# Pool layer of a four-layer trunk: pooled tokens ahead of their row work, bias unsplit, conditioning units redistributed

## The chip, the cores and the metric

One Trainium2 chip, one NeuronCore. The metric is device microseconds of one launch, the median over runs; the kernel before took 1184.72 us (three runs, 1184.19 to 1185.09).

## The reference

The trunk has four layers over x (256 tokens, 1024 channels), all in float32. Layer i mixes tokens by attention (i = 0, 3), a causal convolution (i = 1) or causal pooling (i = 2), and each mixer is followed by a squared-ReLU MLP of 4096 hidden channels:

```python
h = rmsnorm(x) * (1 + scale_a) + shift_a          # rows of c @ ada_w + ada_b
x = x + gate_g * rmsnorm(mixer(h))
h = rmsnorm(x) * (1 + scale_m) + shift_m
x = x + gate_m * rmsnorm(relu(h @ w1) ** 2 @ w2)
# pooling mixer: four groups of 256 channels, windows 2, 4, 8, 16
pooled = trailing_mean(h, window_g) - h
y = (pooled_g @ w_g + b_g) * pool_scale
```

The adaLN rows (shift, scale and gate of every sub-layer) come from one vector c, so each is a matrix-vector product with 1 MB pieces of ada_w.

## The kernel before, in words

Tokens lie as two tiles t = 0, 1 of 128 tokens. Every float32 weight is split into hi and lo halves that TensorE takes at full rate (ACT casts hi, DVE subtracts to lo: `load`, L173 and L174), and a product is three matmuls, hi·hi, lo·hi and hi·lo (`mm3`, L561 to L565). The program runs, for each layer, a mixer and an MLP (`ffn`, 16 chunks). In the middle of MLP chunk 12 (`mid`) some row work of the next layer is issued, such as `shift_rows` (the shift row is transposed into columns, L328 to L341); the pool layer's is not among it.

Between two sub-layers stands `boundary`, a dependent chain. For each tile: ACT sums the squares of y (L135, two halves), POOL makes the reciprocal root r (L119, L121), DVE scales y by the gate row, which was spread over all partitions (`v<-y,bc_g`, L500), adds it to the residual (L505), ACT sums the squares of that (L135), POOL makes the next r, and DVE multiplies by the scale row (`xa<-xs,bc_a`, L358). Then the tile is transposed for the next product; for the pool layer `tokens` multiplies by r and adds the shift instead (L1140). The helper `line` pins these instructions in program order on their engine. On tile 1 the root's first step runs on DVE (L117).

A gate or scale row reaches all partitions in two DMAs on POOL's queue (`spread`): the row to DRAM (`rowd`, L308), then a broadcast read of 512 KB (`bc_g` or `bc_a`, L311).

The adaLN rows are made from "units", one 1 MB piece `araw` each: on TensorE (four matmuls of 512 columns and their weight loads into the bank `adap`, L256) in mixers and boundaries, or on DVE in MLPs (two multiply-adds of 128x1024, L222), whose sums go through `ada_flush` into `adap`. The eighth unit of a row is followed by two DVE row operations (`row`, L231 and L233 or L235). The tables `MIX` and `FF` say how many units each chunk gets, then how many go into the boundary ahead of the sub-layer, then how many pieces are fetched ahead.

`pool` is a stage of its own after its boundary: the remaining unit, the row spread, four bias matmul pairs from a split bias (`ones_r`, L1175, L1176), four groups of products of the tokens with band matrices (`pT_ps`, L1159; tile 1 has a 16-token overlap with tile 0, L1162), copies to hi and lo (`hT<-pT_ps`, L1167 on ACT, L1168 on DVE), and 48 products into y. The order of instructions on each engine comes from a scheduler that follows the dependences, the pinned lines and the `gate` marks.

Of the kernel before, what the change touches and what calls it, by code (L numbers as in the profile page):

```python
# [20 lines left out]
P = 128  # L21
# [30 lines left out]
def tile_trunk(ctx: ExitStack, tc: tile.TileContext, x, cT, pos, invf, ada_w, ada_bg,  # L52
# [150 lines left out]
    def ada(n, vec=()):  # L203
        for _ in range(n):
# [22 lines left out]
            if k == KT - 1:  # L227
                ada_flush(True)
                row = act.tile([P, 512], F32, tag=f"row{g}", name=f"row{g}",
                               bufs=2 if g == 1 else 1)  # L230
                V.tensor_tensor(row, grp["pt"], bg[:, 0], op=ALU.add)  # L231
                if g == 1:
                    V.tensor_tensor(row, row, bg[:, 1], op=ALU.mult)  # L233
                else:
                    V.scalar_tensor_tensor(row[64:], row[64:], 1.0, bg[64:, 1],  # L235
                                           op0=ALU.add, op1=ALU.mult)
                rows[(i, g)] = row
# [86 lines left out]
    def shift_rows():  # L324
        row = bct["sh"]
# [182 lines left out]
    def boundary(ys, units, planes=None, tokens=None):  # L508
        ada(units)
        last.clear()  # L510
# [12 lines left out]
        if not final:  # L523
            r = rsqrt_eps(*cols(ms))
            if tokens is not None:
                tokens(xa, r)
            else:
                bs = transposed0(xa, r)
# [19 lines left out]
        r = rsqrt_eps(*cols(ms), eng=V)  # L548
        if tokens is not None:
            tokens(scaled(1), r)  # L550
        else:
# [3 lines left out]
            for _ in rest:  # L555
                pass
        gate["pool"] = gate["pow"]
# [557 lines left out]
    def pool(i, head, consts, units, ahead):  # L1115
# [13 lines left out]
        def gain_row(raw):  # L1129
            V.tensor_tensor(raw, raw, psc[0:1, :], op=ALU.mult)  # L1130

        for k in range(2):
            fetch(pool_w[j, k])
        fetch(pool_b[j])
        hs = []

# [6 lines left out]
        head(tokens=tokens)  # L1143
        for k in range(2):
            fetch(w1[i, 0, k])
        ada(units)
        wp = [load(pool_w[j, k], gains) for k in range(2)]
        bh, bl = load(pool_b[j], gain_row)
        prep(rows[(i, 2)])
        shift_rows()  # L1150
        bcast("g", rows[(i, 1)], 0)
        ph, pl = planes()
        for t in range(NT):
            for h in range(2):
                b = bank("h", "pT_ps")
                for k in range(4):
                    kk = 4 * h + k
                    ks = slice(kk * P, (kk + 1) * P)
                    T.matmul(b[:, k * P:(k + 1) * P], hs[t][:, ks], band[:, kk // 2, t, 0:P],  # L1159
                             start=(k == 0), stop=(t == 0), skip_group_check=True)  # L1160
                    if t:
                        T.matmul(b[:, k * P:k * P + 16], hs[0][:, ks],  # L1162
                                 band[:, kk // 2, 0, P:P + 16], start=False, stop=True,
                                 skip_group_check=True)
                o = (slice(None), slice(4 * h, 4 * h + 4), slice(t * P, (t + 1) * P))
                b = b.rearrange("p (k t) -> p k t", k=4)
                gate["act"] = A.copy(ph[o], b)  # L1167
                gate["dve"] = V.tensor_tensor(pl[o], b, ph[o].bitcast(F32), op=ALU.subtract)  # L1168
        gate["free"] = 0
        y = y_banks()  # L1170
        for t in range(NT):
            ts = slice(t * P, (t + 1) * P)
            for n in range(2):
                ns = slice(512 * n, 512 * n + 512)
                T.matmul(y[t][n], ones_r, bh[:, ns], start=True, stop=False, skip_group_check=True)  # L1175
                T.matmul(y[t][n], ones_r, bl[:, ns], start=False, stop=False, skip_group_check=True)  # L1176
            for g in range(4):
                for k in range(2):
# [156 lines left out]
```

## Time and profile before

| what | value |
|---|---|
| median of the runs | 1184.72 us |
| profiled execution | 1186.6 us (span 1184.8 us) |
| TensorE (PE) busy | 1139.5 us, 96% |
| DVE, ACT, POOL busy | 844.7, 644.7, 51.8 us |
| mean granted TensorE clock | 0.98 |
| shares of the chain that ended last | PE 62%, DVE 3%, ACT 2%, POOL 1% |

The profile's times run from the span's start. The stages that matter are, in microseconds of the span: first MLP 161 to 344, convolution 352 to 470, second MLP 482 to 667, pool layer 667 to 689.5, its boundary to 698.6, third MLP 698.6 to 884, second attention to 988, last MLP 1003 to the end. A row of a timeline gives start, duration, engine, line, operation, and in brackets how long the engine had idled and what ended that.

### The profile page before, as it was taken

The numbers are of one execution on the slowest core, as the hardware profiler recorded it, in microseconds if no ns is written. First come the engines' busy times: TensorE is split into PE (matmuls) and PEld (weight loads), VectorE is DVE, ScalarE is ACT, GpSimd is POOL, SyncE is SP. The second block draws the span as 40 slices with busy tenths as digits, with TensorE's granted clock in tenths as the row PEclk, the third lists the DMA queues.
The fourth block names the chain that finished last, engine by engine and source line by source line (L and its number), as shares of the span: only waits on it lengthen the run. The fifth ranks groups of instructions, "written<-read, shape, count | busy, mean of one in ns | idle before, by whom it ended". The sixth has DMA issues, their size and how long they took to land.

```text
span 1184.8 us, 17638 instructions
## 1 busy us (share of the span) xinstructions
PE 1139.5 (96%) x6718; PEld 926.0 (78%) x6718; DVE 844.7 (71%) x1197; ACT 644.7 (54%) x1136; POOL 51.8 (4%) x120
## 2 busy tenths in 40 slices
PE   7899989999999999999999999999998999999997
PEld 4667778888878867778788778887877877888886
DVE  3689678777665664768886877787776986655554
ACT  3355565646653243656565566465556665656553
POOL 1000010000010010100000110000011001000000
PEclk9999989999999998999999999999999999999999
DMA  9878757778727783898887568788636432665560
GB/s 331 305 289 309 290 212 269 290 304 296 278 80 249 258 311 139 294 363 318 335 309 291 231 215 317 286 348 331 240 98 222 157 122 74 232 198 190 184 193 36
DMA packets 73385, 290.03 MB, mean 245 GB/s; under 512 B 9986, under 2 KB 15234, under 8 KB 61012
## 3 DMA queue, kind: packets, MB, share of 16 engines
q1 hardware_dynamic: 70484, 280.44, 64.9%
q0 software_dynamic: 2816, 8.46, 2.2%
q8 instruction: 53, 0.87, 0.3%
q14 instruction: 32, 0.26, 0.1%
HBM read 286.57 MB, written 2.29 MB: 244 GB/s over the span
## 4 chain that ended last, share of the span: by engine, by line
PE 62%; DVE 3%; ACT 2%; issue 1%; POOL 1%; DVEq 0%; POOLq 0%; ACTq 0%; DMA 0%
PE h L596 14%; PE y L561 8%; PE y L565 8%; PE y L564 8%; PE h L599 7%; PE dw_ps L1000 3%; PE adap L256 2%; ACT junk L135 1%; PE pw L578 1%; PE pw L584 1%; PE pw L580 1%; POOL r L121 1%; PE hT_ps L395 1%; PE h L578 1%; PE s_ps L913 1%
## 5 line engine op out<-in xcount | busy, mean ns | idle before, releaser
L174 DVE TENSOR_TENSOR lo<-raw,hi 128x1024 fp32r<-128x1024 f32 (+1 forms) x336 | 394.7, 1194 | 114.7 <-ACT hi L173 77.9
L173 ACT CAST hi<-raw 128x1024 fp32r<-128x1024 f32 (+1 forms) x336 | 336.7, 1029 | 94.3 <-PE y L565 55.3
L596 PE MATMUL h<-hT,hi 128*128 128x512 f32 x960 | 240.0, 391 | 0.0
L596 PEld LDWEIGHTS h<-hT,hi 128*128 128x128 f32 x960 | 176.0, 188 | 37.0 <-issue 3.4
L561 PE MATMUL y<-hi,gh 128*128 128x512 f32 x512 | 200.3, 392 | 0.0
L564 PE MATMUL y<-lo,gh 128*128 128x512 f32 x512 | 199.9, 391 | 0.0
L565 PE MATMUL y<-hi,gl 128*128 128x512 f32 x512 | 199.4, 390 | 0.0
L599 PEld LDWEIGHTS h<-hT,lo 128*128 128x128 f32 x960 | 131.0, 190 | 11.8 <-issue 2.5
L599 PE MATMUL h<-hT,lo 128*128 128x256 f32 x960 | 134.5, 283 | 0.0
L646 ACT COPY r<-h 128x256 f32<-128x256 f32 x120 | 44.4, 370 | 159.2 <-PE h L599 158.9
L222 DVE SCALAR_TENSOR_TENSOR acc<-araw,c_act,acc 128x1024 f32<-128x1024 f32 x98 | 120.5, 1280 | 0.0
L565 PEld LDWEIGHTS y<-hi,gl 128*128 128x128 f32 x512 | 96.1, 188 | 23.4 <-issue 2.5
L561 PEld LDWEIGHTS y<-hi,gh 128*128 128x128 f32 x512 | 96.3, 188 | 21.6 <-ACT r L646 1.7
L564 PEld LDWEIGHTS y<-lo,gh 128*128 128x128 f32 x512 | 96.4, 188 | 18.5 <-issue 0.8
L647 DVE TENSOR_TENSOR r<-h,r 128x256 f32<-128x256 f32 x120 | 50.2, 421 | 38.9 <-ACT r L646 38.4
L651 DVE TENSOR_TENSOR gl<-r,gh 128x512 fp32r<-128x512 f32 x64 | 44.2, 690 | 41.7 <-ACT gh L650 41.6
L648 ACT ACTIVATE r<-r 128x512 f32<-128x512 f32 x60 | 38.0, 633 | 33.8 <-DVE r L647 33.6
L500 DVE TENSOR_TENSOR v<-y,bc_g 128x512 f32<-128x512 f32 x32 | 21.8, 687 | 33.4 <-ACT junk L135 23.7
L561 PE MATMUL y<-hi,hT 128*128 128x512 f32 (+1 forms) x112 | 44.1, 402 | 0.0
L565 PE MATMUL y<-hi,hT 128*128 128x512 f32 (+1 forms) x112 | 43.8, 394 | 0.0
L564 PE MATMUL y<-lo,hT 128*128 128x512 f32 (+1 forms) x112 | 43.8, 393 | 0.0
L649 ACT ACTIVATE r<-r 128x512 f32<-128x512 f32 x64 | 40.5, 633 | 1.8
(250 smaller groups left out, 1490.1 us busy)
## 6 DMA issues: line engine op xcount, KB each, us to landing
raw<-in_w_dram SPq DMA_DIRECT2D x256, 512.0 KB
araw<-in_ada_w_dram SPq DMA_DIRECT2D x96, 1024.0 KB
raw<-in_w_pw_dram SPq DMA_DIRECT2D x24, 512.0 KB
raw<-in_w_o_dram SPq DMA_DIRECT2D x16, 512.0 KB
u<-ud SPq DMA_DIRECT2D x32, 132.0 KB
raw<-in_w_ukv_dram SPq DMA_DIRECT2D x8, 512.0 KB
bc_g<-rowd POOLq DMA_DIRECT2D x8, 512.0 KB, 4.9
bc_a<-rowd POOLq DMA_DIRECT2D x7, 512.0 KB, 4.0
```

What stands on the lines that cost most here:

```text
L173: put(A.copy(h, raw), "act")
L174: put(V.tensor_tensor(l, raw, h.bitcast(F32), op=ALU.subtract), "dve")
L222: V.scalar_tensor_tensor(acc, raw[:, sl], ck, acc, op0=ALU.mult, op1=ALU.add)
L561: mm = T.matmul(o, ah, bh, start=start, stop=False, skip_group_check=True)
L564: T.matmul(o, ah, bl, start=False, stop=False, skip_group_check=True)
L565: return T.matmul(o, al, bh, start=False, stop=stop, skip_group_check=True)
L596: T.matmul(b, w(0, kk), pair[:, :, kk], start=(kk == 0), stop=False, skip_group_check=True)
L599: T.matmul(b[:, 0:S], w(1, kk), pair[:, 0, kk], start=False, stop=(kk == KT - 1), skip_group_check=True)
L646: A.copy(rf, hb[:, S:])
L647: V.tensor_tensor(rf, hb[:, 0:S], rf, op=ALU.add)
L649: A.activation(r, r, AF.Square)
L651: gli = V.tensor_tensor(gl, r, gh.bitcast(F32), op=ALU.subtract)
```

## The change

It splits the pool weights ahead of the pool boundary; leaves the bias whole (one float32 matmul per bank, in place of a hi and a lo one); issues the bands of tile 0 as soon as its tokens are known (`early`) with tile 0's y products behind them; puts a product's lo part after all hi parts; moves the pool layer's `shift_rows` into MLP chunk 12; and puts the row operations of units that end in a boundary behind the chain (`defer`, `late`). In the pool layer the root of tile 1 is made on POOL alone. The gate row's spread (`bcast("g", ...)`) is issued ahead of the scale row's (`prep`). Units: pool boundary 3 to 4, pool 1 to 2, boundaries before the second, third MLP and the convolution fewer, attention layer 3 none; the MLPs get one more, one more and two more, one or two to a chunk.

```diff
@@ -226,15 +226,23 @@
                        k == KT - 1 and "acc" not in grp)
             if k == KT - 1:
                 ada_flush(True)
-                row = act.tile([P, 512], F32, tag=f"row{g}", name=f"row{g}",
-                               bufs=2 if g == 1 else 1)
-                V.tensor_tensor(row, grp["pt"], bg[:, 0], op=ALU.add)
-                if g == 1:
-                    V.tensor_tensor(row, row, bg[:, 1], op=ALU.mult)
+                if defer[0] is None:
+                    ada_row(i, g, grp["pt"])
                 else:
-                    V.scalar_tensor_tensor(row[64:], row[64:], 1.0, bg[64:, 1],
-                                           op0=ALU.add, op1=ALU.mult)
-                rows[(i, g)] = row
+                    defer[0].append((i, g, grp["pt"]))
+
+
+    defer = [None]
+
+    def ada_row(i, g, pt, put=lambda eng, ins: ins):
+        row = act.tile([P, 512], F32, tag=f"row{g}", name=f"row{g}", bufs=2 if g == 1 else 1)
+        put("dve", V.tensor_tensor(row, pt, bg[:, 0], op=ALU.add))
+        if g == 1:
+            put("dve", V.tensor_tensor(row, row, bg[:, 1], op=ALU.mult))
+        else:
+            put("dve", V.scalar_tensor_tensor(row[64:], row[64:], 1.0, bg[64:, 1],
+                                              op0=ALU.add, op1=ALU.mult))
+        rows[(i, g)] = row
 
 
 
@@ -321,8 +329,8 @@
         bct["sh"] = row
 
 
-    def shift_rows():
-        row = bct["sh"]
+    def shift_rows(row=None):
+        row = bct["sh"] if row is None else row
         b = bank("h", "sh_ps")
         for k in range(4):
             T.matmul(b[:, 2 * k:2 * k + 2], row[:, k * P:(k + 1) * P], ident[:, 0:33:32],
@@ -505,8 +513,10 @@
             line("dve", V.scalar_tensor_tensor(xs[:, t, sl], v, r, xs[:, t, sl],
                                                op0=ALU.mult, op1=ALU.add))
 
-    def boundary(ys, units, planes=None, tokens=None):
+    def boundary(ys, units, planes=None, tokens=None, early=None):
+        defer[0] = []
         ada(units)
+        late, defer[0] = defer[0], None
         last.clear()
         final = planes is None and tokens is None
         m0, m1 = [sm.tile([P, 2], F32, tag="msy", name="msy") for _ in range(NT)]
@@ -524,6 +534,7 @@
             r = rsqrt_eps(*cols(ms))
             if tokens is not None:
                 tokens(xa, r)
+                low = early()
             else:
                 bs = transposed0(xa, r)
         v1 = [y_scaled(1, ys, 0)]
@@ -545,15 +556,20 @@
         if tokens is None:
             fill0(0)
         ms = squares(1)
-        r = rsqrt_eps(*cols(ms), eng=V)
+        r = rsqrt_eps(*cols(ms), eng=V if tokens is None else None)
         if tokens is not None:
-            tokens(scaled(1), r)
+            xa = scaled(1)
+            low[0]()
+            tokens(xa, r)
+            low[1]()
         else:
             rest = transposed1(r, *planes)
             next(rest)
             fill0(1)
             for _ in rest:
                 pass
+        for a in late:
+            ada_row(*a, line)
         gate["pool"] = gate["pow"]
         gate["free"] = GFREE
 
@@ -1126,13 +1142,14 @@
             gains.n += 1
         gains.n = 0
 
-        def gain_row(raw):
-            V.tensor_tensor(raw, raw, psc[0:1, :], op=ALU.mult)
-
         for k in range(2):
             fetch(pool_w[j, k])
         fetch(pool_b[j])
+        wp = [load(pool_w[j, k], gains) for k in range(2)]
+        bias = fetched.pop((pool_b[j].tensor.name, pool_b[j].offset))
+        V.tensor_tensor(bias, bias, psc[0:1, :], op=ALU.mult)
         hs = []
+        ph, pl = planes()
 
         def tokens(xa, r):
             for h in range(2):
@@ -1140,62 +1157,79 @@
                 line("dve", V.scalar_tensor_tensor(xa[:, sl], xa[:, sl], r, shb[:, sl],
                                                    op0=ALU.mult, op1=ALU.add))
             hs.append(xa)
-        head(tokens=tokens)
+
+
+
+        def means(t, h, b=None):
+            if b is None:
+                b = bank("h", "pT_ps")
+                for k in range(4 if t else 0):
+                    kk = 4 * h + k
+                    T.matmul(b[:, k * P:k * P + 16], hs[0][:, kk * P:(kk + 1) * P],
+                             band[:, kk // 2, 0, P:P + 16], start=(k == 0), stop=False,
+                             skip_group_check=True)
+                if t and len(hs) == 1:
+                    return b
+            for k in range(4):
+                kk = 4 * h + k
+                T.matmul(b[:, k * P:(k + 1) * P], hs[t][:, kk * P:(kk + 1) * P],
+                         band[:, kk // 2, t, 0:P], start=(t == 0 and k == 0), stop=True,
+                         skip_group_check=True)
+            o = (slice(None), slice(4 * h, 4 * h + 4), slice(t * P, (t + 1) * P))
+            b = b.rearrange("p (k t) -> p k t", k=4)
+            gate["act"] = line("act", A.copy(ph[o], b))
+
+            def low():
+                gate["dve"] = line("dve", V.tensor_tensor(pl[o], b, ph[o].bitcast(F32),
+                                                          op=ALU.subtract))
+            return low
+
+        ahead1 = []
+
+        def early():
+            low = [means(0, h) for h in range(2)]
+            ahead1.append(means(1, 0))
+            return low
+
+        head(tokens=tokens, early=early)
         for k in range(2):
             fetch(w1[i, 0, k])
+        for low in [means(1, 0, ahead1[0]), means(1, 1)]:
+            low()
+        gate["free"] = 0
+        bcast("g", rows[(i, 1)], 0)
+        prep(rows[(i, 2)])
         ada(units)
-        wp = [load(pool_w[j, k], gains) for k in range(2)]
-        bh, bl = load(pool_b[j], gain_row)
-        prep(rows[(i, 2)])
-        shift_rows()
-        bcast("g", rows[(i, 1)], 0)
-        ph, pl = planes()
-        for t in range(NT):
-            for h in range(2):
-                b = bank("h", "pT_ps")
-                for k in range(4):
-                    kk = 4 * h + k
-                    ks = slice(kk * P, (kk + 1) * P)
-                    T.matmul(b[:, k * P:(k + 1) * P], hs[t][:, ks], band[:, kk // 2, t, 0:P],
-                             start=(k == 0), stop=(t == 0), skip_group_check=True)
-                    if t:
-                        T.matmul(b[:, k * P:k * P + 16], hs[0][:, ks],
-                                 band[:, kk // 2, 0, P:P + 16], start=False, stop=True,
-                                 skip_group_check=True)
-                o = (slice(None), slice(4 * h, 4 * h + 4), slice(t * P, (t + 1) * P))
-                b = b.rearrange("p (k t) -> p k t", k=4)
-                gate["act"] = A.copy(ph[o], b)
-                gate["dve"] = V.tensor_tensor(pl[o], b, ph[o].bitcast(F32), op=ALU.subtract)
-        gate["free"] = 0
         y = y_banks()
         for t in range(NT):
             ts = slice(t * P, (t + 1) * P)
             for n in range(2):
-                ns = slice(512 * n, 512 * n + 512)
-                T.matmul(y[t][n], ones_r, bh[:, ns], start=True, stop=False, skip_group_check=True)
-                T.matmul(y[t][n], ones_r, bl[:, ns], start=False, stop=False, skip_group_check=True)
-            for g in range(4):
-                for k in range(2):
-                    a, b = wp[g // 2]
-                    ws = slice((2 * (g % 2) + k) * 256, (2 * (g % 2) + k) * 256 + 256)
-                    kk = 2 * g + k
-                    mm3(y[t][g // 2][:, 256 * (g % 2):256 * (g % 2) + 256], ph[:, kk, ts],
-                        pl[:, kk, ts], a[:, ws], b[:, ws], start=False, stop=(k == 1))
+                T.matmul(y[t][n], ones_f[0:1], bias[:, 512 * n:512 * n + 512], start=True,
+                         stop=False, skip_group_check=True)
+            for low in range(2):
+                for g in range(4):
+                    for k in range(2):
+                        ws = slice((2 * (g % 2) + k) * 256, (2 * (g % 2) + k) * 256 + 256)
+                        for q in ((0, 1), (0,))[low]:
+                            T.matmul(y[t][g // 2][:, 256 * (g % 2):256 * (g % 2) + 256],
+                                     (ph, pl)[low][:, 2 * g + k, ts], wp[g // 2][q][:, ws],
+                                     start=False, stop=(low == 1 and k == 1),
+                                     skip_group_check=True)
         return y
 
 
 
     MIX = {
         0: ([2, 4, 2, 3, 3, 2], 0, 1),
-        1: ([0, 0, 2, 0, 1, 2, 1, 0, 1], 3, 4),
-        2: (1, 3, 3),
-        3: ([0, 2, 0, 0, 0, 0], 0, 0),
+        1: ([0, 0, 2, 0, 1, 2, 1, 0, 1], 2, 3),
+        2: (2, 4, 3),
+        3: ([0, 0, 0, 0, 0, 0], 0, 0),
     }
     FF = {
-        0: ([1, 2, 1, 0, 2, 0, 3, 0, 2, 2, 0, 0, 0, 1, 0, 0], 1, 3),
-        1: ([1, 1, 0, 1, 2, 2, 1, 2, 2, 2, 1, 0, 0, 1, 0, 0], 4, 3),
-        2: ([0, 2, 0, 2, 0, 3, 1, 1, 2, 0, 2, 0, 1, 3, 0, 1], 3, 0),
-        3: ([0, 0, 0, 0, 0, 0, 0, 0, 0, 0, 0, 0, 0, 0, 0, 0], 0, 0),
+        0: ([1, 1, 1, 1, 1, 2, 1, 1, 1, 1, 1, 1, 1, 1, 0, 0], 1, 3),
+        1: ([1, 1, 1, 2, 1, 1, 2, 1, 1, 2, 1, 1, 1, 1, 0, 0], 2, 4),
+        2: ([1, 1, 1, 1, 2, 1, 2, 1, 2, 1, 1, 2, 1, 2, 1, 0], 2, 0),
+        3: ([0] * NFC, 0, 0),
     }
     qgs = cp.tile([P, q_g.shape[0], 3], F32, name="qgs")
     kgs = cp.tile([P, kv_g.shape[0], 2], F32, name="kgs")
@@ -1236,6 +1270,7 @@
                     if i % 3 == 1:
                         nonlocal consts
                         consts = pool_consts(pool_p, (i + 1) // 3)
+                        shift_rows(rows[(i + 1, 2)])
                 y = ffn(i, (hi, lo), sched[0], sched[2], mid)
             else:
                 y = (mla if i % 3 == 0 else conv)(i, (hi, lo), sched[0], sched[2])
```

**POOL, around the pool layer.** `v<-msy` and `r<-v,mhalf` are the root of a y tile of the boundary that follows the row's DMAs; `row_6346` and `row_6447` are the gate row, `row_5556` and `row_5643` the scale row. Before:

```order
L121 TENSOR_TENSOR r<-v,mhalf 128x1 x3
L308 DMA rowd<-row_5556 2x512
L308 DMA rowd<-row_6346 2x512
L311 DMA bc_a<-rowd 128x1024
L311 DMA bc_g<-rowd 128x1024
L119 TENSOR_SCALAR v<-msy 128x1
L121 TENSOR_TENSOR r<-v,mhalf 128x1
```

Now:

```order
L121 TENSOR_TENSOR r<-v,mhalf 128x1
L316 DMA rowd<-row_6447 2x512
L316 DMA rowd<-row_5643 2x512
L119 TENSOR_SCALAR v<-msy 128x1
L121 TENSOR_TENSOR r<-v,mhalf 128x1
L319 DMA bc_g<-rowd 128x1024
L319 DMA bc_a<-rowd 128x1024
```

The two broadcast reads have moved behind the root of the next boundary's tile 0, and the gate row's is now the first of them.

**DVE, from the tokens of tile 0 to the next boundary** (`xa<-xa,r,shb` are the tokens). Before:

```order
L1140 SCALAR_TENSOR_TENSOR xa<-xa,r,shb 128x512 x2
L500 TENSOR_TENSOR v<-y_4853,bc_g 128x512
L174 TENSOR_TENSOR lo<-raw,hi 1x1024
...
L505 SCALAR_TENSOR_TENSOR xs<-v,r,xs 128x512
L231 TENSOR_TENSOR row_6346<-adap,bg 128x512
L505 SCALAR_TENSOR_TENSOR xs<-v,r,xs 128x512
L233 TENSOR_TENSOR row_6346<-row_6346,bg 128x512
...
L1140 SCALAR_TENSOR_TENSOR xa<-xa,r,shb 128x512 x2
```

Now:

```order
L174 TENSOR_TENSOR lo<-raw,hi 128x1024
L1157 SCALAR_TENSOR_TENSOR xa<-xa,r,shb 128x512 x2
...
L1183 TENSOR_TENSOR hT<-pT_ps,hT 128x4x128
L1157 SCALAR_TENSOR_TENSOR xa<-xa,r,shb 128x512 x2
L1183 TENSOR_TENSOR hT<-pT_ps,hT 128x4x128
L239 TENSOR_TENSOR row_6447<-adap,bg 128x512
L241 TENSOR_TENSOR row_6447<-row_6447,bg 128x512
L1183 TENSOR_TENSOR hT<-pT_ps,hT 128x4x128 x2
L508 TENSOR_TENSOR v<-y_6492,bc_g 128x512
```

The gate row's two operations have moved from between the residual halves of tile 1 to behind its tokens.

**ACT, the same stretch** (`junk,msy<-y` and `junk,ms<-xs` are the sums of squares; `hi<-raw 128x1024` are here casts of the third MLP's first weights). Before:

```order
L135 ACTIVATE junk,msy<-y_4852 128x512
L135 ACTIVATE junk,ms<-xs 128x512 x2
L173 CAST hi<-raw 1x1024
L135 ACTIVATE junk,msy<-y_4853 128x512
L173 CAST hi<-raw 128x1024
L135 ACTIVATE junk,msy<-y_4854 128x512
L173 CAST hi<-raw 128x1024
```

Now:

```order
L135 ACTIVATE junk,msy<-y_4837 128x512
L173 CAST hi<-raw 128x1024
L135 ACTIVATE junk,ms<-xs 128x512
L173 CAST hi<-raw 128x1024
L135 ACTIVATE junk,ms<-xs 128x512
L135 ACTIVATE junk,msy<-y_4838 128x512
L1180 CAST hT<-pT_ps 128x4x128 x2
L135 ACTIVATE junk,msy<-y_4839 128x512
```

The two casts have moved ahead of and between the squares of tile 0, and the copies of tile 0's bands ahead of the last squares of y.

## Rows read from the trace of the kernel before

**Rows 1.** Window, first MLP: length; busy PE, PEld, DVE, ACT, POOL; clock, DMA.

```profile
167.00:343.00 176.00, 176.00 (x900) 147.70 (x899) 131.81 (x146) 103.03 (x152) 2.00 (x4) 1.00 0.74 275
```

**Rows 2.** Timeline of DVE, pool stage: start, us, line, operation.

```profile
667.02 1.42 DVE L1140 SCALAR_TENSOR_TENSOR xa<-xa,r,shb 128x512 f32<-128x512 f32 x2 [0.84 <-POOL r L121]
...
672.87 0.69 DVE L233 TENSOR_TENSOR row<-row,bg 128x512 f32<-128x512 f32 x1
...
675.24 1.41 DVE L1140 SCALAR_TENSOR_TENSOR xa<-xa,r,shb 128x512 f32<-128x512 f32 x2
...
687.17 1.29 DVE L500 TENSOR_TENSOR v<-y,bc_g 128x512 f32<-128x512 f32 x2 [1.92 <-DMA bc_g<-rowd]
688.62 1.42 DVE L505 SCALAR_TENSOR_TENSOR xs<-v,r,xs 128x512 f32<-128x512 f32 x2 [0.16 <-POOL r L121]
```

**Rows 3.** Timeline of POOL, pool stage and the boundary behind it.

```profile
675.08 1.18 POOL L308 DMA_DIRECT2D rowd<-row  x2
680.49 0.57 POOL L311 DMA_DIRECT2D bc_a<-rowd  x1 [4.23 <-DVE hT L1168]
681.05 0.54 POOL L311 DMA_DIRECT2D bc_g<-rowd  x1
...
688.02 0.56 POOL L121 TENSOR_TENSOR r<-v,mhalf 128x1 f32<-128x1 f32 x1
```

**Rows 4.** Timeline of PE and ACT after that boundary.

```profile
692.08 0.40 ACT L371 ACTIVATE dg<-ident,r 128x128 f32<-128x128 f32 x1 [0.42 <-POOL r L121]
...
698.58 0.39 PE L578 MATMUL h<-hT,hi 128*128 128x256 f32 x1
```

**Rows 5.** Timeline of ACT, end of the second MLP and pool boundary.

```profile
661.78 0.60 ACT L135 ACTIVATE junk<-y 128x512 bf16<-128x512 f32 x1 [0.28 <-PE y L565]
...
667.31 1.03 ACT L173 CAST hi<-raw 128x1024 fp32r<-128x1024 f32 x1
668.25 0.58 ACT L135 ACTIVATE junk<-y 128x512 bf16<-128x512 f32 x1
...
673.87 0.59 ACT L1167 CAST hT<-pT_ps 128x512 fp32r<-128x512 f32 x1
```

**Rows 6.** Tile view of bc_g: time from issue to landing.

```profile
DMA to landing us min/median/max: 3.6/4.9/9.5
```

**Rows 7.** Timeline of PE, pool stage.

```profile
666.83 2.78 PE L256 MATMUL adap<-araw,c_act 128*32 128x512 f32 x24
...
671.31 0.83 PE L1159 MATMUL pT_ps<-band,xa 128*128 128x128 f32 x6
...
674.66 0.49 PE L1175 MATMUL y<-hi,ones_r 1*128 1x512 f32 x1
674.99 0.38 PE L1176 MATMUL y<-lo,ones_r 1*128 1x512 f32 x1
...
689.34 0.28 PE L565 MATMUL y<-hi,hT 128*128 128x256 f32 x1
```

**Rows 8.** Windows, columns as in rows 1: two idle stretches, two slow ones.

```profile
149.00:153.00 4.00, 2.71 (x15) 1.09 (x13) 3.50 (x6) 1.43 (x4) 0.00 (x0) 1.00 0.83 339
153.20:163.60 10.40, 8.26 (x33) 6.98 (x34) 7.12 (x16) 5.48 (x17) 3.08 (x6) 0.52 0.06 19
...
679.40:686.05 6.65, 6.65 (x32) 6.65 (x33) 3.49 (x4) 1.28 (x3) 1.10 (x2) 0.50 0.94 322
...
695.30:697.80 2.50, 0.02 (x1) 0.01 (x1) 1.50 (x5) 0.95 (x4) 1.13 (x2) 1.00 1.03 421
```

**Rows 9.** Timeline of PE: flushes, shift columns, units of the second attention.

```profile
332.03 1.06 PE L256 MATMUL adap<-acc,ones_c 128*32 128x512 f32 x8
...
522.41 1.05 PE L256 MATMUL adap<-acc,ones_c 128*32 128x512 f32 x4
...
836.58 0.95 PE L328 MATMUL sh_ps<-ident,row 128*128 128x2 f32 x8
...
914.26 1.07 PE L256 MATMUL adap<-araw,c_act 128*32 128x512 f32 x8
```

## The prediction

> **What bounds the kernel now.** I read the stages first, then the chain around the pool layer, then what each boundary waits for last. In the MLPs TensorE is busy for the whole of the window, in the first one 176.00 of 176.00 us, while DVE is busy for 131.81 of them [rows 1]. So a more even spread of DVE units there has no wait to remove, and I cost it at nothing; TensorE's own work covers it. Between the sub-layers the kernel hangs on short dependent instructions. Behind the pool layer, DVE waits 1.92 us for the gate row's broadcast until 687.17, but the first residual starts at 688.62, 0.16 us after DVE was free, when POOL's root is done: the root, not the broadcast, came last [rows 2, 3]. From that residual the chain runs through the diagonal of tile 0 at 692.08 to the first product of the third MLP at 698.58, which is 9.96 us later [rows 2, 4]. I take this stretch as a constant: whatever moves the residual moves the third MLP.
>
> **The change, part by part.** The profiled execution took 1186.6 us, 1.9 more than the median of 1184.72; the terms below are differences, and I set them against both.
>
> *The pool boundary, tile 0.* In the changed order the last product of the first bank of y stands 19 matmuls before the MLP's end, where it stood 27 before; the second bank likewise has moved by 8. At 0.23 us for one matmul of 512 columns (2.78 us for twelve, [rows 7]) tile 0's squares start 1.8 us later. One weight cast, 1.03 us [rows 5], now stands between the two squares of the residual. The tokens of tile 0 therefore start near 669.85 instead of 667.02 [rows 2], +2.8.
>
> *The pool boundary, tile 1.* The last square of y, at 668.25 before [rows 5], now stands behind the two copies of tile 0's bands. Those copies need the bands, which need the tokens; six band matmuls take 0.83 us [rows 7], the copies 0.59 each [rows 5], and so that square starts near 673.55. From there square (0.7), root, residual (1.42), squares (1.4) and root follow with less between them than before: gone are the row operations and the bias's 1.2 us on DVE. I get the tokens of tile 1 at 678.5 instead of 675.24 [rows 2], +3.3. The root that moves from DVE to POOL adds 0.15 of it.
>
> *The row work.* It sat between the residuals and ended by 673.56; the two row DMAs were issued at 675.08 and the broadcasts at 680.49 and 681.05 [rows 2, 3]. Now tokens (1.41), one copy's subtraction (0.69) and two row operations (0.69 each) follow one another on DVE: they end at 682.0. POOL then issues two row DMAs (1.18 us [rows 3]), and behind them stands the root of the next boundary's tile 0, and only behind that root the gate broadcast. This is the term that decides. On TensorE the second bands run from 679.9 to 682.1, two units (0.23 us a matmul) and the last products of tile 0 end at 684.55; one square (0.60 and its readout) and the root (0.30 and 0.56) add 1.9, so the broadcast is issued at 686.5, 5.4 us later than before. It lands 3.6 to 9.5 us after issue, 4.9 in the median [rows 6]; the one it replaces took 6.1 (681.05 to 687.17, [rows 2, 3]), with another broadcast ahead of it. I take 4.9, as it is now the first of the two: it lands at 691.4, two products with it take 1.29, and the residual starts at 692.7 instead of 688.62: **+4.1**, with +2.8 at 3.6 and +8.7 at 9.5. By the Trainium skill ("DMA: Bandwidth & Descriptors", section "Anatomy of one DMA — SWDGE (gpsimd) path") a DMA takes a fixed 2.0 us plus its bytes at 436 GB/s, which as an estimate is 3.2 us for 512 KB and a term of +2.4; the trace has no gate broadcast that quick, its fastest took 3.6 [rows 6].
>
> *Other work in the pool stage.* The weight splits move ahead of the head but were hidden, DVE and ACT being idle for some of the MLP's last chunks. The unsplit bias takes two casts out of the chains (counted) and puts four float32 matmuls in place of eight. The eight take 0.33 us each from start to start [rows 7], 2.6 in all. The trace has no float32 matmul of one row over 128 output rows; the nearest are the adaLN ones, float32 with 512 columns and 32 output rows, of which the four of a unit take 0.93 (2.78 for twelve, [rows 7]). If one of full height takes as long as one of these, four cost 0.9; if as long as the four together, 3.7. I take 3.4, near the dear end. It lies under the wait for tile 1's tokens. The y products end near 687.4, before 689.5 [rows 7], though the stage gains nothing from it: the broadcast is later.
>
> *The granted clock.* Before, 6.65 us of the pool stage ran at 0.50, the 1.2 GHz level, which is about 3.3 us lost [rows 8]; I assume the denser order holds 2.4 GHz there, and have the 3.3 us in the times above. In the following boundary TensorE now idles for some 6 us. The trace has both answers to idling: 2.5 us without work at 695.3 and the clock stayed at 1.00, but the broadcast wait around 149 was followed by 10.4 us at 0.52, which reached 2.5 us into the first MLP [rows 8]. The longer idle is nearer to the second: **+1.25** (2.5 us at half), bounds 0 and 3.3.
>
> *TensorE in the MLPs.* The first MLP's last flush is now issued in two halves, and a half takes as long as a whole one, 1.05 against 1.06 [rows 9]: **+1.0**. The shift columns of the pool layer move into chunk 12 of the second MLP, where TensorE has no free time: **+0.9**, as 0.95 in the third MLP [rows 9]. Flushes of the other MLPs keep their number.
>
> *The second attention.* Its two units and their row work go. One unit took 1.07 us in a full stretch of TensorE [rows 9]; two give −2.1 if nothing waits underneath, and the DVE row operations up to −1.4 more. As the stage is bound by DVE in places, **−1.8**, bounds 0 and −3.5.
>
> *The boundaries of convolution, second and third MLP.* They lose units, but a unit there fills idle time; 0, bounds −1 and +1.
>
> Sum: 4.1 + 1.25 + 1.0 + 0.9 − 1.8 = **+5.45**. From the profiled 1186.6 that is 1192.1, from the median **1190.2 us**. Its own range is 1186 (3.6 us broadcast, full clock, the most for the attention) to 1195 (landing as slow as the 9.5). A difference of 0.2%, about 2.4 us, is what a measurement of this kernel can tell from none.
>
> **Rivals.** *No change.* If tile 1's chain is not held up by ACT's copies (tokens at 675.24 still), the row work ends at 678.7, tile 0's y at 682.0 and its root at 683.9; at 3.6 us the broadcast lands at 687.5 and the residual starts at 688.8, the old place. The rest gives +0.1 to +0.5: 1185. For it: ACT's copies may come earlier than I have them. Against: four dependent estimates must all be too long.
>
> *Faster.* The shorter TensorE work sets the end: y ends 2.1 us earlier and the boundary follows it. This needs the broadcast to land before 685.2 (the old residual's 688.62 less 2.1 and 1.29), so its issue by about 681, and the attention must give −3.5. Then −2.1 + 1.9 − 3.5 = −3.7, 1181.0. Against it is that POOL's order puts the issue behind a root that needs all of tile 0's y.
>
> *Slower still.* TensorE waits for the tokens of tile 1 and the clock falls in the pool stage as before: +3.3 more, 1193.5. For it: 6.65 us at 0.50 with TensorE busy throughout [rows 8]. By the Trainium skill, "TensorE: Matmul & The Clock Gate", Part 1, the throttled level is the default and activity releases it, so each wait that the new order adds would speak for this one; that the clock fell here without an idle stretch shows the rule does not settle it.
>
> **How the numbers follow.** Likeliest case 0.53, slower still 0.12, no change 0.17, faster 0.18. So slower 0.65, same 0.17, faster 0.18. The range from 1181 to 1195 takes in the first three, the bounds of the dear terms and the faster case's slower half.
>
> **What would show it.** Right: in the profile after, the row of `v<-y,bc_g` behind the pool layer starts near 691 with idle time ended by the broadcast's DMA, POOL's issue of bc_g stands behind the root near 686, and the first product of the third MLP is about 4 us later measured from the second MLP's end. Wrong: that first `v<-y,bc_g` is released by ACT's squares and starts before 687, or the third MLP's start has come nearer to the second's end; then the estimate of tile 1's chain or of the landing has failed. The flush, the shift columns and the attention are each read by their own stage's length.

## The result and the profile after

The changed kernel took 1200.3 us in the median (1196.12 to 1206.88, four runs) against 1184.45 for the kernel before: a ratio of 1.0135, 95% interval 1.0093 to 1.0177. It is slower, as forecast, but by 15.9 us and not by 5.5, and above the range. The profiled execution took 1198.78 us (span 1197.0), 12.2 more than the one of before; the rows and stages below account for these 12.2.

The mechanism of the prediction is there. The first product with the gate row behind the pool layer is released by the broadcast's DMA. On POOL the broadcast stands behind the root of tile 0 and starts when that root is done, as forecast. But it lands 9.3 us after its issue (688.00 to 697.31), where I took 4.9. Timeline of DVE after, the rows that answer to [rows 2]:

```profile
677.61 1.41 DVE L1157 SCALAR_TENSOR_TENSOR xa<-xa,r,shb 128x512 f32<-128x512 f32 x2 [0.25 <-POOL r L121]
...
680.25 0.69 DVE L241 TENSOR_TENSOR row<-row,bg 128x512 f32<-128x512 f32 x1
...
697.31 1.29 DVE L508 TENSOR_TENSOR v<-y,bc_g 128x512 f32<-128x512 f32 x2 [12.50 <-DMA bc_g<-rowd]
698.52 1.41 DVE L513 SCALAR_TENSOR_TENSOR xs<-v,r,xs 128x512 f32<-128x512 f32 x2
```

Timeline of POOL after, for [rows 3]:

```profile
681.24 1.18 POOL L316 DMA_DIRECT2D rowd<-row  x2 [3.66 <-DVE row L241]
687.09 0.29 POOL L119 TENSOR_SCALAR v<-msy 128x1 f32<-128x1 f32 x1 [4.67 <-ACT junk L135]
687.47 0.56 POOL L121 TENSOR_TENSOR r<-v,mhalf 128x1 f32<-128x1 f32 x1
688.00 0.63 POOL L319 DMA_DIRECT2D bc_g<-rowd  x1
```

What the rows of before left out is the queue of SP, the engine that issues the loads of weights and adaLN pieces. Timeline of SP, the kernel before:

```profile
667.96 2.04 SPq L196 DMA_DIRECT2D araw<-in_ada_w_dram  x3
670.10 0.91 SPq L155 DMA_DIRECT2D raw<-in_w_dram  x2
673.48 17.52 SPq L196 DMA_DIRECT2D araw<-in_ada_w_dram  x2
691.05 0.54 SPq L199 DMA_DIRECT2D bg<-in_ada_bg_dram  x1
691.64 1.46 SPq L155 DMA_DIRECT2D raw<-in_w_dram  x3
```

and after (rows of two windows):

```profile
667.12 2.90 SPq L196 DMA_DIRECT2D araw<-in_ada_w_dram  x4
...
684.73 0.33 SPq L196 DMA_DIRECT2D araw<-in_ada_w_dram  x1
685.15 0.87 SPq L155 DMA_DIRECT2D raw<-in_w_dram  x2
686.12 0.56 SPq L196 DMA_DIRECT2D araw<-in_ada_w_dram  x1
686.73 0.54 SPq L199 DMA_DIRECT2D bg<-in_ada_bg_dram  x1
687.32 1.45 SPq L155 DMA_DIRECT2D raw<-in_w_dram  x3
```

A piece `araw` is 1 MB, a weight `raw` 0.5 MB. A row of SP that covers two issues runs from the start of the first to the end of the second: of the two pieces in the row of 673.48, the second went out at 690.7. A new piece may only come when TensorE has used the old one, and SP issues in order, so the weights behind it wait too. Before, the next such piece and the weights went out at 690.7 to 693, behind the broadcast. After, the two units inside the pool layer, which use two adaLN pieces at 683.6,

```profile
683.60 1.92 PE L264 MATMUL adap<-araw,c_act 128*32 128x512 f32 x16
```

release 4.5 MB between 684.7 and 688.8. I call this the pile. The broadcast, issued at 688.0, has to share the 16 DMA engines with it. The windows after show them full from the issue to the landing, at 348 to 421 GB/s (last two columns: DMA share, GB/s; the column before is the granted clock):

```profile
680.00:684.00 4.00, 4.00 (x23) 3.53 (x25) 1.60 (x3) 1.09 (x3) 1.18 (x2) 0.57 0.01 2
684.00:688.00 4.00, 4.00 (x37) 2.81 (x30) 0.69 (x1) 1.36 (x5) 0.83 (x3) 1.00 0.56 178
688.00:692.00 4.00, 3.54 (x27) 1.57 (x26) 0.00 (x0) 0.00 (x0) 1.18 (x3) 1.00 1.03 421
692.00:696.00 4.00, 0.00 (x0) 0.00 (x0) 0.00 (x0) 0.00 (x0) 0.00 (x0) 0.73 0.99 348
696.00:700.00 4.00, 0.00 (x0) 0.00 (x0) 2.69 (x5) 0.65 (x2) 0.00 (x0) 0.50 1.02 417
```

As an estimate, at some 420 GB/s the 4.5 MB and the two broadcasts (0.5 MB each) take 13 us, from 685 to 698; by the windows some 4.3 MB had moved when the gate's broadcast landed at 697.3, so it waited for most of the pile, if not for all. The Trainium skill says this in one line ("Trainium Kernel Development and Optimization", section "Key Constraints"): DMAs from SP's, ACT's and POOL's queues run on the same 16 engines and interleave. The trace agrees in that the broadcast on POOL's queue took 9.3 us beside SP's 4.5 MB, and 4.1 to 6.1 us in the kernels that had little or nothing of SP's left to move.

The MLPs grew too. In the second MLP a product waits for an ACT cast, in the third a flush waits for DVE's sums; before, no product in an MLP waited. The first MLP's last flush is now two, as forecast. Timeline of PE after:

```profile
316.07 1.05 PE L264 MATMUL adap<-acc,ones_c 128*32 128x512 f32 x4
317.06 0.73 PE L612 MATMUL h<-hT,hi 128*128 128x512 f32 x2
317.72 1.05 PE L264 MATMUL adap<-acc,ones_c 128*32 128x512 f32 x4
...
617.73 0.95 PE L336 MATMUL sh_ps<-ident,row 128*128 128x2 f32 x8
...
643.48 1.20 PE L577 MATMUL y<-hi,gh 128*128 128x512 f32 x4 [1.52 <-ACT hi L173]
...
665.99 3.64 PE L264 MATMUL adap<-araw,c_act 128*32 128x512 f32 x32
...
672.74 1.98 PE L1207 MATMUL y<-raw,ones_f 1*128 1x512 f32 x4
...
708.94 0.58 PE L594 MATMUL h<-hT,hi 128*128 128x256 f32 x1
...
880.59 1.05 PE L264 MATMUL adap<-acc,ones_c 128*32 128x512 f32 x4 [1.60 <-DVE acc L222]
```

The 12.2 us of the profiled execution by stage (first product of an MLP to its last, and what lies between):

| stage | before | after | difference |
|---|---|---|---|
| first MLP | 183.2 | 185.2 | +2.0 |
| convolution with its boundaries | 138.3 | 132.1 | −6.2 |
| second MLP | 184.4 | 187.8 | +3.4 |
| its end to the third MLP's first product | 31.75 | 42.95 | +11.2 |
| third MLP | 185.9 | 188.3 | +2.4 |
| second attention with its boundaries | 114.9 | 114.6 | −0.3 |
| last MLP | 179.15 | 178.9 | −0.25 |

The gain in the convolution has two parts. The boundary ahead of the second MLP, which lost two units, takes 7.6 us instead of 9.3; so it does in every kernel below with the new tables (7.6 to 7.7), while those with the old ones take 9.2 and 9.3. The rest is the granted clock: window 340 to 480 has a mean of 0.95 before and 0.98 after, and a stretch of 13 us near 0.50 from 440 is missing after. Whether the tables do that too is not shown, but it is no mere chance of one profile: the convolution with its boundaries takes 129.4 to 133.1 us in all eleven profiles with the new tables, and 135.4, 138.3 and 143.1 us in the three with the old.

### The profile page after: what moved, and what is told of

The parts are those of the page before. It is cut to its first block, busy times and chain, and to the rows that moved or that the text cites. A ratio compares the mean times of both kernels' runs of the same rounds, so it can differ in the third digit from the quotient of the medians.

```text
span 1197.0 us, 17571 instructions
## 1 busy us (share of the span) xinstructions
PE 1136.0 (95%) x6686; PEld 927.6 (77%) x6686; DVE 852.3 (71%) x1203; ACT 643.7 (54%) x1135; POOL 52.3 (4%) x121
## 4 chain that ended last, share of the span: by engine, by line
PE 57%; DVE 4%; ACT 3%; issue 2%; DMA 2%; POOL 1%; SPq 0%; DVEq 0%; POOLq 0%; ACTq 0%
PE h L612 13%; PE y L577 8%; PE y L580 8%; PE y L581 8%; PE h L615 7%; PE dw_ps L1016 2%; ACT junk L135 1%; PE adap L264 1%; PE pw L594 1%; PE pw L600 1%; PE pw L596 1%; DMA raw<-in_w_pw_dram 1%; POOL r L121 1%; PE hT_ps L403 1%; DVE lo L174 1%
## 5 line engine op out<-in xcount | busy, mean ns | idle before, releaser
L174 DVE TENSOR_TENSOR lo<-raw,hi 128x1024 fp32r<-128x1024 f32 (+2 forms) x335 | 393.2, 1193 | 107.0 <-ACT hi L173 74.2
L173 ACT CAST hi<-raw 128x1024 fp32r<-128x1024 f32 (+2 forms) x335 | 335.3, 1029 | 89.9 <-PE y L581 46.7
L222 DVE SCALAR_TENSOR_TENSOR acc<-araw,c_act,acc 128x1024 f32<-128x1024 f32 x106 | 130.7, 1278 | 0.0
L666 ACT CAST gh<-r 128x512 fp32r<-128x512 f32 x64 | 39.7, 620 | 1.5
L577 PE MATMUL y<-hi,hT 128*128 128x512 f32 x96 | 38.0, 397 | 0.0
L135 ACT ACTIVATE junk<-xs 128x512 bf16<-128x512 f32 x32 | 20.2, 631 | 32.6 <-DVE xs L513 29.3
```

What stands on the lines that cost most here:

```text
L173: put(A.copy(h, raw), "act")
L174: put(V.tensor_tensor(l, raw, h.bitcast(F32), op=ALU.subtract), "dve")
L222: V.scalar_tensor_tensor(acc, raw[:, sl], ck, acc, op0=ALU.mult, op1=ALU.add)
L577: mm = T.matmul(o, ah, bh, start=start, stop=False, skip_group_check=True)
```

## The experiments

The kernels below ran in four groups on three chips of the same kind. There the kernel before took 1185.6 to 1187.1 in the median, and a single run of it 1178 to 1194; each ratio below is to the kernel before in its own group. Single profiles are read by their waits and not by their totals. "Stretch" is the time from the first adaLN product behind the second MLP to the third MLP's first product, 31.75 before and 42.95 after; beside it stands the mean granted clock in that stretch, 0.89 and 0.79. The stretch follows that clock as well as the waits, so its differences of 2 or 3 us say little; the time from the broadcast's issue to its use on DVE is the surer reading.

**The changed kernel again.** 

> The changed kernel once more, on the chip of the other runs of this batch, so that it can be compared with them. Theory E (the new tables let SP issue about 3.5 MB more ahead of the broadcast, which lands only when that pile is through): 1196 to 1203, and the broadcast again lands 8 us or more after its issue. If the first runs were a bad draw of the granted clock: 1190 to 1194.

1199.82 us, ratio 1.0121 (1.0068 to 1.0175): the loss is not a draw. The broadcast is issued at 694.71, and DVE starts with it at 703.53, 8.8 us later; stretch 47.2, clock 0.70. In this profile TensorE, busy throughout, had a granted clock of 0.50 from 676.3 to 689.7, and the issue came 4.8 us later after the second MLP than in the first profile of the changed kernel.

**POOL's order alone.** A dependence holds the root behind the broadcasts:

```diff
+            if gate.get("root") is not None:
+                nosync(add, gate["root"])
```

> The changed kernel with one thing else: the root of the next boundary's tile 0 on POOL is pinned behind the gate broadcast, so the broadcast no longer waits for the sums of y. Theory A (issue behind the root, then sharing the DMA engines with 4.5 MB that SP issues from 684.7): the broadcast is issued when the row has landed, near 684, lands by 689 to 691, and the third MLP starts 6 to 8 us earlier than in the changed kernel; about 1190 us. Theory B (the row operations behind the chain are what is late): issue still after 687, no change, about 1199.

1189.1 us, ratio 1.0019 (0.9992 to 1.0046). The broadcast is issued at 680.70, as soon as the row has landed, after 0.83 us of waiting for that, and the root decides again; the stretch is 36.9 (clock 0.80), though 12 us of it ran at half clock:

```profile
672.00:684.00 12.00, 12.00 (x40) 8.68 (x40) 6.12 (x10) 1.45 (x4) 3.21 (x6) 0.50 0.46 188
```

Theory A holds, B falls: the row was there in time. But this edit removes both conditions at once: the two units end later here, SP's pile goes out from 687.4 only, and the broadcast has no transfers beside it. Order and sharing are told apart by the next runs.

**The units alone, behind y.** `ada(units)` moved from ahead of `y_banks()` to the end of `pool`. 

> The changed kernel with the pool layer's two adaLN units issued behind the y products; POOL's order is kept. SP's transfers that wait for those units then start at about 688 instead of 684.7, and y of tile 0 is done 1.9 us earlier, so the broadcast is issued near 686. Theory A: with a head start on the other transfers it lands in 4 to 5.5 us, near 691, the third MLP starts 5 to 7 us earlier; about 1192. Theory C (the broadcast is slow by itself, whatever runs beside it): it again takes 9 us, lands near 695; about 1196.

1191.39 us, ratio 1.0046 (1.0012 to 1.0079). POOL's order is that of the changed kernel, SP's pile goes out from 684.8, behind the broadcast, and this lands in 4.6 us (POOL, then DVE); stretch 36.6, clock 0.84:

```profile
682.07 0.56 POOL L121 TENSOR_TENSOR r<-v,mhalf 128x1 f32<-128x1 f32 x1
682.60 0.63 POOL L319 DMA_DIRECT2D bc_g<-rowd  x1
```

```profile
687.21 1.29 DVE L508 TENSOR_TENSOR v<-y,bc_g 128x512 f32<-128x512 f32 x2 [6.20 <-DMA bc_g<-rowd]
```

So the broadcast is not slow by itself; C falls. The units moved behind y give back more than half of the loss, with POOL's order as it was.

**The row work not behind the chain.** `defer[0] = [] if tokens is None else None`. 

> The changed kernel with the two row operations of the pool boundary not put behind the chain; they fall back between the residual's instructions, and in the order on POOL both broadcasts then stand ahead of the root again. Theory A: rows done near 675, broadcast issued by 681, landed by 688, so POOL's root decides again: the third MLP starts about 9 us earlier than in the changed kernel; about 1189. Theory D (the half clock and the second MLP explain most of the loss): less than 4 us regained, about 1195.

1191.83 us, ratio 1.006 (1.0038 to 1.0082): the forecast of 1189 missed. The broadcast is issued ahead of the root, at 680.42, and yet lands at 688.84, 8.4 us later; stretch 37.5, clock 0.87. In this order the units run at 671 and 674, so the pile is let go earlier and lies ahead of the broadcast. An early issue is no help when it goes into the pile.

**The tables alone, in the old code.** 

> The kernel before with only the new tables of units; the pool layer's code is the old one. Theory A: the broadcasts stand ahead of the root as before, so the pool boundary keeps its length; the first MLP's flush costs 1.0, the attention gains up to 1.8: 1183 to 1186. Theory D (the redistribution itself costs): 1190 or more, with the loss in the second MLP.

1193.8 us, ratio 1.0073 (1.0045 to 1.0102): A's forecast of no loss falls. Theory D's total of 1190 or more came, but not its place: the second MLP has only 1.8 us of the loss. The old code with the new tables has the broadcasts ahead of the root, and the wait is as long (SP, POOL, DVE):

```profile
662.05 7.31 SPq L196 DMA_DIRECT2D araw<-in_ada_w_dram  x5
669.45 1.79 SPq L155 DMA_DIRECT2D raw<-in_w_dram  x2
673.35 0.33 SPq L196 DMA_DIRECT2D araw<-in_ada_w_dram  x1
673.73 0.54 SPq L199 DMA_DIRECT2D bg<-in_ada_bg_dram  x1
674.31 1.94 SPq L155 DMA_DIRECT2D raw<-in_w_dram  x3
```

```profile
678.26 0.54 POOL L311 DMA_DIRECT2D bc_g<-rowd  x1
```

```profile
689.19 1.29 DVE L500 TENSOR_TENSOR v<-y,bc_g 128x512 f32<-128x512 f32 x2 [10.16 <-DMA bc_g<-rowd]
```

8.5 MB leave SP between 662 and 676, where before it was 5 MB by 674; as an estimate, at 420 GB/s that lasts to about 684, the broadcasts share the end of it, and 10.9 us pass from issue to use; stretch 39.8, clock 0.85. This gave theory E: what counts is how much SP has let go when the broadcast starts.

**The old tables in the new code.** 

> The changed kernel's code with the old tables of units: the pool boundary has three units, the pool layer one. In its order the broadcast still stands behind the root of the next boundary's tile 0. Theory E: the pile is as small as before, so the broadcast lands 4 to 5.5 us after issue although it is issued late; the pool-to-MLP stretch is 3 to 5 us longer than before and not 11; the MLPs lose only the shift columns' 1.0; about 1188. Theory A (POOL's order is the cause, the tables are not): as the changed kernel, 1195 or more.

The edit also issues the pool layer's one unit ahead of the broadcast. The broadcast stands behind the root, is issued at 695.06 and used at 699.89, 4.8 us: as E has it, and the very case that I had predicted. The stretch is 38.1 (clock 0.82), +6.3, where I had +5.35 (4.1 and 1.25). But the total, 1195.14 (four runs, ratio 1.0096, 1.0053 to 1.0138), is what theory A had and not E's 1188, and its interval overlaps that of the changed kernel: the old tables alone do not give the loss back. In this profile the convolution with its boundaries takes 143.1 us (window 340 to 480: clock 0.94), 4.8 more than before, the second attention 2.4 more, and the three MLPs 1.1 to 1.6 more each. I cannot settle how much of that belongs to the code.

**One unit fewer in the pool layer, tables otherwise new, old code.** `2: (1, 4, 3)` and a boundary of 3 behind it. 

> The kernel before with the new tables, but one unit of the pool layer moved behind it into the next boundary (pool 1, boundary 3). The broadcasts fall behind the root in POOL's order here. Theory E: the pile ahead of the broadcast is smaller by one piece and the weights that SP holds behind it, about 2.5 MB, so it lands within 6 us of its issue, and the stretch from the pool layer's y to the third MLP is 3 to 7 us shorter than with the new tables (21.4 us there); about 1188. Theory F (something else in the tables delays it): landing again 9 us or more, 1193.

1187.35 us, ratio 1.0018 (0.9993 to 1.0043). The three last weights and a piece now leave at 687.5 and later; the broadcast takes 5.3 us (681.90 to 687.23), stretch 33.8 against 39.8. The broadcasts had even fallen behind the root in POOL's order. POOL, DVE and the window of the issue:

```profile
681.90 0.55 POOL L311 DMA_DIRECT2D bc_g<-rowd  x1
```

```profile
687.23 1.29 DVE L500 TENSOR_TENSOR v<-y,bc_g 128x512 f32<-128x512 f32 x2 [4.27 <-DMA bc_g<-rowd]
```

```profile
680.00:684.00 4.00, 4.00 (x25) 2.64 (x24) 1.38 (x2) 1.03 (x2) 1.66 (x3) 1.00 0.98 350
```

The DMA engines were full at the issue here, 0.98, yet the landing was quick: SP had issued nothing since 675, and little was left to move. One unit in the wrong place costs 6 us of the stretch here, part of it through the clock (0.98 in this stretch, 0.85 with the unit).

**Uneven lists.** The MLPs' lists in the old shape with the new sums. 

> The kernel before with the new tables, but the MLPs' lists in the old uneven shape with the new sums (15, 17 and 20 units). Theory G (the even lists make TensorE wait at a flush: 1.5 us in the second MLP for ACT's cast, 1.6 to 2.4 in the third for DVE's sums): these waits go, 2 to 4 us less than with the new tables, about 1190. If the extra units themselves cause the waits: they stay, 1193.

1190.78 us, ratio 1.0035 (1.0008 to 1.0062), 3 us below the new tables, though the two intervals overlap. The third MLP's wait is gone (its length 187.3 against 189.8), the second's 1.52 for ACT's cast stays. So in the old code the one wait goes with the even list; the other comes with the extra units or the moved flush, which no run tells apart. The broadcast lands 10.4 us after issue, as the pile is untouched.

**No unit inside the pool layer, the rest as changed.** `2: (0, 4, 3)` and a boundary of 4. 

> The changed kernel with no unit inside the pool layer: both go into the boundary behind it (pool 0, boundary 4). POOL's order stays, the broadcast behind the root. Theory E: nothing that SP holds is let go before y is done, so the broadcast lands 4 to 5 us after its issue instead of 9; from the second MLP's end to the third MLP's first product 35 to 38 us where the changed kernel had 43 and 47; 1189 to 1193. Theory A (order alone): still 41 or more, 1197.

1192.29 us, ratio 1.0056 (1.0032 to 1.008). Landing in 4.3 us (685.96 to 690.26), as E has it, and the total is within E's forecast; the stretch is 39.5, above the forecast, with a clock of 0.78 in it, where the kernel with one unit had 0.98.

**Both undone.** The same with the dependence of the experiment on POOL's order. 

> Both undone in the changed kernel: no unit inside the pool layer and the root pinned behind the broadcasts. The broadcast then neither waits for y nor shares the DMA engines. Theory E with A's order as the second part: the root decides, 31 to 34 us from the second MLP's end to the third's first product, 1185 to 1189; what is left over the kernel before is the MLPs' waits and the shift columns (4 to 5 us). If a third thing delays the boundary: 36 or more.

1187.85 us, ratio 1.0018 (0.9997 to 1.004). The broadcast takes 4.1 us from issue to use (683.80 to 687.87). Stretch 32.6, clock 0.92: in this profile the loss at the boundary is gone but for 0.9 us.

**Both undone and the lists uneven.** 

> Both undone as in the run before (no unit in the pool layer, the root behind the broadcasts), and the MLPs' lists in the old uneven shape with the new sums. Theory G: the third MLP's wait at its last flush (1.1 to 2.4 us) goes, the second MLP's 1.5 stays, as it did with the old lists in the old code: 1 to 2 us faster than with the even lists, 1185 to 1187, which the noise of these runs can hardly tell from the kernel before. If the lists play no part: 1188.

1188.36 us, ratio 1.001 (0.9986 to 1.0035), no measurable difference to the run before. The wait in the third MLP has moved, not gone: it is 2.69 us at the first flush, at 743.8, instead of 1.1 at the last. The pool layer is that of the run before, and yet the stretch is 35.4, with a clock of 0.81: 2.8 us between two profiles of the same instructions there.

**No unit inside the pool layer, in the kernel before.** 

> The kernel before with no unit inside the pool layer (pool 0, its boundary 4), nothing else. Theory E: with the last row finished in the boundary and no transfer let go in the middle, the stretch from the second MLP's end to the third's first product is 1 to 3 us shorter than before; 0 to 3 us faster than the kernel before. If the unit there was hidden: no difference.

1185.46 us, ratio 0.9999 (0.9976 to 1.0022): no difference: a unit moved out of the pool layer changes nothing there that these runs can tell. The stretch did not shorten as E had forecast: it is 34.9, with a clock of 0.80. No version here beats the kernel before.

## Why the prediction missed

- **The broadcast behind the root: mechanism right, size wrong.** This is the failed term: the landing time, and with it the issue. Up to the row work the working held: tile 1's tokens start 11.5 us behind the second MLP's end where it had 11.6, and the row operations end at 14.9 where it had 15.1. Then I had the broadcast issued 19.7 us behind the first adaLN product that follows the second MLP; it was 22.0. And I had it land 4.9 us after issue, by the median of [rows 6]; it took 9.3 and 8.8. The residual came 10.7 us later instead of 4.1, and from it to the third MLP's first product 10.4 us passed where I had taken 9.96 as a constant. The working took a landing time from other places of the program and asked only what stands ahead in POOL's queue. I listed the units that move into the pool layer by their time on TensorE (1.9 us) and not by the DMAs that their end releases on SP. Five kernels with no pile, or little left of it, show 4.1 to 5.3 us, five with it 8.4 to 10.9. The fixed-plus-bytes rule of the Trainium skill ("DMA: Bandwidth & Descriptors", section "Anatomy of one DMA — SWDGE (gpsimd) path"), which I had cited, gave 3.2; no landing here was that quick.
- **The warning stood in the trace of before.** The 9.5 us at the top of [rows 6], which I priced as a bound, is the broadcast behind the first attention, beside 4.5 MB that SP issues in 5.3 us, with a DMA share of 0.94 to 1.01. SP, POOL and DVE, the kernel before:

```profile
136.80 1.45 SPq L155 DMA_DIRECT2D raw<-in_w_dram  x2
138.29 0.90 SPq L196 DMA_DIRECT2D araw<-in_ada_w_dram  x2
139.29 2.84 SPq L155 DMA_DIRECT2D raw<-in_w_dram  x3
```

```profile
139.89 0.56 POOL L311 DMA_DIRECT2D bc_g<-rowd  x1 [4.38 <-DMA rowd<-row]
```

```profile
149.50 1.29 DVE L500 TENSOR_TENSOR v<-y,bc_g 128x512 f32<-128x512 f32 x2 [7.72 <-DMA bc_g<-rowd]
```

- **Full clock in the pool stage: wrong.** I assumed that the denser order holds 2.4 GHz there. From 680.3 to 683.6 the clock was 0.50 with TensorE busy. As an estimate these 3.3 us cost 1.6, most of the 2.3 by which the issue came late; in the second profile of the changed kernel it was 13 us.
- **The clock behind it: +1.25, about right.** The clock fell to 0.50 at 694, while TensorE idled for 10.9 us where I had some 6, and stayed there until 710.9, over the boundary's chain and 2 us of the third MLP. The chain came out 0.5 us longer; half of the 2 us is 1, as an estimate.
- **"A more even spread has no wait to remove, and I cost it at nothing": wrong.** There was no wait to remove, but one to add: 1.52 us in the second MLP, 1.60 in the third. The three MLPs gave +7.8 where I had +1.9. The flush (+1.0) and the shift columns (0.95) came as forecast; some 2.7 us are in neither of these nor in the waits.
- **The boundaries of convolution, second and third MLP at 0: wrong for one.** The one ahead of the second MLP is 1.7 us shorter, outside the bounds of −1 and +1: its two units were not all hidden.
- **The second attention, −1.8: not borne out.** −0.3 in these two profiles. The eleven profiles without its units have 114.0 to 115.1 us, the three with them 114.9, 117.2 and 118.7; whether the units were hidden is not settled.
- **The bias: about right.** Two float32 matmuls of one row take 1.9 us (672.74 to 674.65), four 3.8, just past the dear end of my bounds. That they were hidden is not shown: the bands of tile 1 start at 680.0, a microsecond after its tokens were done, with TensorE busy until then.
- **Sum.** The stretch +11.2 instead of +5.35 and the MLPs +7.8 instead of +1.9 explain the miss; in the profiled execution 6.2 us came back in the convolution, which I had not counted on. The medians lie 3.7 us further apart than the two profiles; no stage is known for that part.

"The slower still" rival had the half clock in the pool stage, which came in part, and fell short too. The runs show half-clock stretches of 12 us in the pool layer in some kernels (the experiment on POOL's order, with TensorE busy throughout) and none in others (0.98 over the whole stretch with one unit fewer); what sets them is open.

What is shown and what is not: that SP's transfers delay the broadcast rests on ten landing times, and that waiting for it costs the boundary rests on the kernels that removed the wait (ratios of 1.0018 to 1.0056 against 1.0121 and 1.0135). How much of the total goes to the order, to the pile and to the clock is not separated, and the old tables in the new code (1.0096) do not fit a count by the pile alone.

## What to carry to other kernels

When work that consumes a prefetched buffer is moved, follow what its end lets go on the DMA queue: here one 1 MB unit more in the pool layer released 2.5 MB more in front of a small transfer that the critical chain needed, and the transfer waited for most of it. A landing time read elsewhere in the trace is only good where as few bytes are ahead as there; count what the queue has issued and the engines have not moved at the time of issue. The DMA share alone does not tell: it was 1.03 just behind the issue in the changed kernel (9.3 us) and 0.98 at the issue with one unit fewer (5.3 us). And an engine at 80% over an MLP (DVE, 150.8 of 188.3 us in the third) still makes a flush wait where its list of work ends just ahead of it.

## What I had not expected of the hardware

A 512 KB broadcast took 4.1 to 5.3 us from issue to use with little or nothing of another queue's transfers left to move, and 8.4 to 10.9 us behind 4.5 to 8.5 MB of them, although its own queue held nothing but the other broadcast. The place and the length of the half-clock stretches change from kernel to kernel, also where the instructions are the same: 13 us from 440, in the convolution, in the kernel before and none there in the changed one, which is most of the 6 us that came back there.
